# First feed-forward products over plain quarters, later conversions, and a gate product on VectorE

## The chip, the cores and the metric

The kernel runs on one core of one Trainium2 chip. The metric is the device time of one execution in microseconds. The figure for the kernel before is the median of three runs; the profile is of one more execution, with a time of its own.

## What is computed

The reference runs one inference step of a four-part decoder trunk on 1024 prompt rows and 64 sample rows (8 sequences of 8) of width 1024, in float32:

```python
for i in range(DEPTH):                       # DEPTH = 2
    mix = rglru_mixer(x, ...) if i % 2 == 0 else hgrn2_mixer(x, ...)
    x = layer_norm(ALPHA * x + mix, ln_g[i, 0], ln_b[i, 0])
    f = conv_ffn(x, ffn_conv[i], ffn_w_in[i], ffn_conv_w[i], ffn_conv_b[i], ffn_w_out[i])
    x = layer_norm(ALPHA * x + f, ln_g[i, 1], ln_b[i, 1])

def conv_ffn(x, buf, w_in, cw, cb, w_out):   # w_in is 1024 x 5632
    gate, up = jnp.split(x @ w_in, 2, axis=-1)
    gc, new_buf = causal_dwconv(gate, buf, cw, cb)
    return (jax.nn.gelu(gc) * up) @ w_out, new_buf

# in rglru_mixer, of 1024 channels in 8 heads of 128:
    r = jax.nn.sigmoid(gates[0]); ig = jax.nn.sigmoid(gates[1])
    log_a = RG_C * r * jax.nn.log_sigmoid(lam)
    a = jnp.exp(log_a)
    bvals = jnp.sqrt(jnp.maximum(-jnp.expm1(2.0 * log_a), 0.0)) * ig * xc
    _, h = lax.associative_scan(combine, (a, bvals), axis=1)
```

## The kernel before

**Numbers in two halves.** Every float32 operand of a product is kept as a high half (a cast by ScalarE, ACT in the profile) and a low half (the value minus the high half, a subtraction on GpSimd, POOL, or on VectorE, DVE). A product of two such operands is three products on TensorE (PE): high by high, high by low, low by high.

**Four phases.** Phase 0 is the RG-LRU mixer with its out-projection, phase 1 the first feed-forward layer, phase 2 the HGRN2 mixer, phase 3 the second feed-forward layer. `ffn` builds phases 1 and 3 with the same code. In the profile the start of phase 1 lies at about 348 us and that of phase 3 at about 1804 us, the same rows 1455.7 us later.

**The program is a list of steps** (`stepf`). Each step names weight blocks and a function. `blocks` holds all weight blocks in the order of use, and two things run ahead of the products along it. `issue_raw` starts loads of float32 weights into free raw buffers (raw0, raw1, in a feed-forward layer rawf0, rawf1 too), on SyncE's queue (SP); L140 is the load. `convert` turns what is loaded into high and low halves in a weight tile (wb0, wb1, wb2, wxf0, each of two halves). A raw buffer returns to `rawq` when the conversion of its whole block is written. `pump`, which `products` and `ln_pipeline` call, writes such conversions and pending work into the program; so the place of a conversion in each engine's queue is decided when the program is written, and every engine takes its queue in order.

**In-projection of a feed-forward layer.** Steps alternate: `gates` of a pair of 128-column blocks (f0, f1), then `ups` of the same pair. `products` multiplies a pair by a scheme of seven products over quarters: the rows of x are cut in two halves of 512, the inner dimension in two halves of 512, the pair in its two blocks. The seven left sides are sums and differences of quarters of x, xc[0] to xc[6], of which xc[0], [3], [4] and [6] are used by the change. The seven right sides are sums and differences of weight quarters, made by `convert_part`: four of the seven parts need one more subtraction or addition on POOL (L176, L178, L180, L182) before the cast (L185) and the low half (L186). Each product is 12 matmuls (4 inner tiles by 3), and is done for two chunks of rows, c = 0 with n = 288 (256 prompt rows and 32 sample rows) and c = 1 with n = 256. That is 2 x 7 x 12 = 168 matmuls for a pair. In a first pair, `order` in `products` takes all seven products of c = 0 ahead of those of c = 1; in later ones the two chunks alternate. Results go from PSUM to row-long slots by copies on ACT and additions on DVE in `evac` (L1103, L1110, L1118).

**How x comes to its quarters.** `ln_pipeline` runs over nine row tiles in the order 8, 0, 4, 1, 5, 2, 6, 3, 7 (8 holds the sample rows): the last out-projection products of the tile, then `pump()`, then in `nrm_a` the square of the centred rows on ACT (L455) with its sum, then on DVE the scale and shift. `to_sums(mp)` for mp = 0 to 3 transposes the tiles mp and mp + 4 on PE (L375) and makes xc of them: ACT writes the high halves (L402), POOL three of the low ones (L406), and in `late()` POOL subtracts (L427), ACT casts and POOL subtracts again for xc[5]. Chunk c = 0 needs mp 0 and 1, chunk c = 1 needs mp 2 and 3. The last one, `to_sums(3)`, is left pending, and `flush` writes it into the middle of the first pair's products.

**RG-LRU.** For each of eight heads `rg_a`, `rg_b`, `rg_c` follow one another in `pend`: on ACT exponential and tanh, on DVE L873, L875 and L876 over 128 x 1112 elements, on ACT the square root L882, on POOL the product of input gate and convolved row L883 (in `rg_b`), on DVE its product with the square root L893, then the scans L900 and L901.

**Last out-projection group of a feed-forward layer.** Four weight blocks of 256 rows x 512 columns: (f0, columns 0), (f0, columns 1), (f0+2, columns 0), (f0+2, columns 1). They are converted by `convert` with their low halves on the engine that `run["lo"]` names (POOL in these phases, L217).

## Time and profile before

| | |
|---|---|
| median of 3 runs | 2586.22 us (2585.59 to 2587.18) |
| profiled execution, its own time | 2582.2 us |
| span in the profile | 2580.4 us |
| PE busy in the span | 2492.6 us, 97% |
| DVE, ACT, POOL busy | 1551.0, 955.3, 1415.4 us |
| mean granted clock of TensorE | 0.989 of full speed |

The profiled execution is 4.0 us shorter than the median, and its span 1.8 us shorter than its time. PE is idle for 88 us of the span. In the chain that ended last, PE's products have the greatest shares, and DVE, POOL and ACT together 7%.

### The profile page before, as it was taken

Reading aid. Unit: us, or ns where it says so; the run is one execution under the profiler, and the core shown is the slowest. Engines: PE = TensorE matmul, PEld = TensorE weight load, DVE = VectorE, ACT = ScalarE, POOL = GpSimd, SP = SyncE. Lnnn points to the kernel's source line nnn. Section 1 sums busy time; section 2 is a strip of 40 time slices with the busy share of each in tenths; the row PEclk is TensorE's granted clock in tenths of the full one; section 3 lists DMA queues with packets and bytes.
Section 4 is the critical chain, followed back from the end, with each engine's and each line's share of the span. In section 5 each row is a group of like instructions: output and inputs, shape, how many; then the busy total and the mean of one; then the engine's idle time right before and its main releaser. Section 6 shows DMA issues by size and latency. Waiting matters only on the chain. (4 is left out here: it accounts for less than half of the span.)

```text
span 2580.4 us, 39885 instructions
## 1 busy us (share of the span) xinstructions
PE 2492.6 (97%) x16007; PEld 2306.8 (89%) x16007; DVE 1551.0 (60%) x2367; ACT 955.3 (37%) x1653; POOL 1415.4 (55%) x1179
## 2 busy tenths in 40 slices
PE   9999979999999999999999999999799999999997
PEld 9998869999999788799999999877799999988886
DVE  5998375665655422468858485977556565662327
ACT  4776243333333211244545353444333333340113
POOL 2664168888886532115544453614788888872321
PEclk9999989999999999999999999999999999999999
DMA  4114121222224422121211111122222222264112
GB/s 133 41 46 149 50 82 59 80 80 85 67 85 146 177 101 84 48 83 42 60 34 50 51 43 51 43 93 97 74 85 67 85 67 89 71 243 142 61 38 73
DMA packets 205839, 209.79 MB, mean 81 GB/s; under 512 B 13201, under 2 KB 167953, under 8 KB 205614
## 3 DMA queue, kind: packets, MB, share of 16 engines
q1 hardware_dynamic: 205654, 207.25, 25.0%
q8 instruction: 126, 2.06, 0.3%
q14 instruction: 59, 0.48, 0.1%
HBM read 159.61 MB, written 47.61 MB: 80 GB/s over the span
## 5 line engine op out<-in xcount | busy, mean ns | idle before, releaser
L217 POOL TENSOR_TENSOR wb<-raw,wb 128x1024 fp32r<-128x1024 f32 (+1 forms) x76 | 202.4, 2666 | 493.3 <-ACT wb L216 273.2
L1103 DVE TENSOR_TENSOR z<-z,ps_f 128x256 f32<-128x256 f32 (+2 forms) x550 | 195.9, 378 | 363.6 <-PE ps_f L1098 295.0
L1098 PE MATMUL ps_f<-xa,wb 128*128 128x288 f32 (+1 forms) x3072 | 397.5, 289 | 11.6 <-POOL wb L186 4.7
L1098 PEld LDWEIGHTS ps_f<-xa,wb 128*128 128x128 f32 x3072 | 390.1, 188 | 14.2 <-POOL wb L186 5.6
L1098 PE MATMUL ps_f<-x,wb 128*128 128x288 f32 (+1 forms) x2496 | 325.6, 291 | 0.3 <-ACT z L1110 0.3
L1098 PEld LDWEIGHTS ps_f<-x,wb 128*128 128x128 f32 x2496 | 321.2, 190 | 1.1 <-ACT z L1110 1.1
L300 PE MATMUL ps_in<-xa,wb 128*128 128x384 f32 (+3 forms) x912 | 307.4, 337 | 13.2 <-ACT y8h L1391 5.9
L301 PE MATMUL ps_in<-xa,wb 128*128 128x384 f32 (+3 forms) x912 | 300.5, 330 | 0.3 <-DVE xa L358 0.3
L302 PE MATMUL ps_in<-xa,wb 128*128 128x384 f32 (+3 forms) x912 | 300.5, 329 | 0.1
L444 DVE SCALAR_TENSOR_TENSOR z<-z,ps_fo 128x512 f32<-128x512 f32 x128 | 87.4, 685 | 290.3 <-PE ps_fo L1203 281.7
L186 POOL TENSOR_TENSOR wb<-rawf,wb 128x512 fp32r<-128x512 f32 x116 | 165.6, 1436 | 57.0 <-ACT wb L185 55.5
L186 POOL TENSOR_TENSOR wb<-raw,wb 128x512 fp32r<-128x512 f32 x116 | 162.9, 1410 | 60.6 <-ACT wb L185 50.4
L300 PEld LDWEIGHTS ps_in<-xa,wb 128*128 128x128 f32 x912 | 173.6, 190 | 17.9 <-ACT y8h L1391 7.3
L1151 DVE SCALAR_TENSOR_TENSOR z<-z,ptf 128x1104 f32<-128x1104 f32 x88 | 182.3, 2071 | 1.6
L301 PEld LDWEIGHTS ps_in<-xa,wb 128*128 128x128 f32 x912 | 173.6, 190 | 1.3 <-DVE xa L358 0.7
L302 PEld LDWEIGHTS ps_in<-xa,wb 128*128 128x128 f32 x912 | 173.2, 190 | 1.1 <-DVE wb L217 0.5
L216 ACT CAST wb<-raw 128x1024 fp32r<-128x1024 f32 (+1 forms) x81 | 79.7, 986 | 233.7 <-issue 117.5
L1098 PE MATMUL ps_f<-xa,wxf 128*128 128x256 f32 (+1 forms) x1152 | 149.8, 288 | 2.4 <-ACT z L1118 2.4
L1098 PEld LDWEIGHTS ps_f<-xa,wxf 128*128 128x128 f32 x1152 | 146.6, 188 | 2.8 <-ACT z L1118 2.8
L185 ACT CAST wb<-rawf 128x512 fp32r<-128x512 f32 x116 | 71.0, 623 | 208.2 <-POOL rawf L182 76.0
L185 ACT CAST wb<-raw 128x512 fp32r<-128x512 f32 x116 | 70.4, 624 | 187.2 <-POOL raw L182 63.7
L1201 PE MATMUL ps_fo<-wb,xa 128*128 128x512 f32 x320 | 126.4, 395 | 2.4 <-DVE z L444 2.4
(510 smaller groups left out, 5710.9 us busy)
## 6 DMA issues: line engine op xcount, KB each, us to landing
raw<-in_ffn_w_in_dram SPq DMA_DIRECT2D x44, 512.0 KB
rawf<-in_ffn_w_in_dram SPq DMA_DIRECT2D x44, 512.0 KB
ysave<-z SPq DMA_DIRECT2D x44, 512.0 KB
raw<-in_hg_w_in_dram SPq DMA_DIRECT2D x32, 512.0 KB
xa<-ysave SPq DMA_DIRECT2D x28, 544.0 KB
zsave<-z SPq DMA_DIRECT2D x24, 512.0 KB
raw<-in_ffn_w_out_dram SPq DMA_DIRECT2D x24, 512.0 KB
z<-zsave SPq DMA_DIRECT2D x24, 512.0 KB
```

The lines of the kernel that those rows point to most:

```text
L185: act.copy(w[:, 0], src)
L186: run["lo"].tensor_tensor(w[:, 1], src, w[:, 0], ALU.subtract)
L216: act.copy(w[:, 0, :n], raw[:, :n])
L217: run["lo"].tensor_tensor(w[:, 1, :n], raw[:, :n], w[:, 0, :n], ALU.subtract)
L300: pe.matmul(ps[:, :n], lhsT=wh, rhs=xh, start=(k == 0), stop=False)
L301: pe.matmul(ps[:, :n], lhsT=wh, rhs=xl, start=False, stop=False)
L302: pe.matmul(ps[:, :n], lhsT=wl, rhs=xh, start=False, stop=(k == KT - 1))
L444: dve.scalar_tensor_tensor(zz, zz, a, ps, ALU.mult, ALU.add, accum_out=stat[:, m, n:n + 1] if acc else None)
L1098: pe.matmul(ps[:, :n], lhsT=l, rhs=r, start=(kk == 0 and i < 4 and l is wh and r is xh), stop=(kk == 3 and l is wl), skip_group_check=(i > ...
L1103: dve.tensor_tensor(d, s, pv(ps), ALU.add)
L1151: dve.scalar_tensor_tensor(c[:, :L], gs[:, i:i + L], w[:, i:i + 1], c[:, :L], ALU.mult, ALU.add)
L1201: pe.matmul(ps, lhsT=yh, rhs=wh, start=a, stop=False)
```

## The change

1. **First gates block of each feed-forward layer.** It has the kind "q": four parts, which are its four quarters as they are. `products_first` multiplies them by xc[0], xc[3], xc[4], xc[6] in eight products for each chunk, 192 matmuls for the pair in place of 168. Within a chunk it does f0 whole and then f1. For each of both, xc[0] and xc[3] meet the first quarter in two PSUM banks, then xc[4] and xc[6] meet the second quarter in the same two banks. The first bank is copied to its place after the first product and again after the third, and the second bank is added after the fourth. `flush` comes after f0 of chunk 0.
2. **Place of conversions.** In the last tile of `ln_pipeline` `pump()` stands behind `nrm_a` and `late()`. In the second pass of the mixer's out-projection a call of `convert()` is taken out.
3. **`rg_b`.** The product of input gate and convolved row is on DVE.
4. **Last out-projection group.** The blocks stand in the order (f0, columns 0), (f0+2, columns 0), (f0, columns 1), (f0+2, columns 1), and the low halves that are made at the end of the group before are on DVE.
5. `products` loses its argument `first`.

```diff
@@ class Block @@
+            self.parts = 1 if len(loads) == 1 else 4 if kind == "q" else 7
@@ convert_part @@
-        if i == 1:
+        if b.parts == 4:
+            src = (a11, a12, a21, a22)[i]
+        elif i == 1:
             pool.tensor_tensor(a21, a11, a21, ALU.subtract)
...
@@ ln_pipeline @@
         for i, m in enumerate(order):
             step_m(m)
-            pump()
+            if i < NT - 1:
+                pump()
             nrm_a(m, junk())
             late()
+            if i == NT - 1:
+                pump()
@@ mix_out, second pass @@
-                        if n == 1:
-                            convert()
@@ rg_b @@
-        pool.tensor_tensor(ig[:, :W], ig[:, :W], st["xc"][:, :W], ALU.mult)
+        dve.tensor_tensor(ig[:, :W], ig[:, :W], st["xc"][:, :W], ALU.mult)
@@ ffn @@
+        def products_first(b, places):
+            for f, (get, pieces) in enumerate(places):
+                get()
+            for c in range(2):
+                c0, n = HCH[c]
+                for f, (get, pieces) in enumerate(places):
+                    q1, q2 = pieces(0, c), pieces(1, c)
+                    banks = [psi.tile([P, 512], F32, name="ps_f", tag="in") for _ in range(2)]
+                    for h, xs in enumerate(((0, 3), (4, 6))):
+                        while len(b.w) <= 2 * f + h:
+                            assert convert(), "no place for weights"
+                        w = b.w[2 * f + h][0]
+                        for ps, i in zip(banks, xs):
+                            for kk in range(4):
...
+                                    pe.matmul(ps[:, :n], lhsT=l, rhs=r, start=(h == 0 and kk == 0 and l is wh and r is xh),
+                                              stop=(kk == 3 and l is wl), skip_group_check=(h == 1))
+                            if i == 0:
+                                for d, pv in q2:
+                                    act.copy(d, pv(ps))
+                            elif i == 4:
+                                for d, pv in q1:
+                                    act.copy(d, pv(ps))
+                            elif i == 6:
+                                for d, pv in q2:
+                                    dve.tensor_tensor(d, d, pv(ps), ALU.add)
+                        pump()
+                    if c == 1:
+                        put_half(b.w[2 * f][1])
+                        put_half(b.w[2 * f + 1][1])
+                        pump()
+                    if c == 0 and f == 0:
+                        flush()
...
-            order = [(i, c) for c in range(2) for i in range(7)] if first else [(i, c) for i in range(7) for c in range(2)]
-            for i, c in order:
+            for i, c in [(i, c) for i in range(7) for c in range(2)]:
...
+                            if gi + 2 == len(GROUPS):
+                                run["lo"] = dve
...
                     flush()
+                    run["lo"] = pool
...
-                        prod(m, 0, grp, [ws[0], ws[2]], False, True)
+                        prod(m, 0, grp, ws[:2], False, True)
...
-                stepf(phase, [out_blk(WO, f0, 0), out_blk(WO, f0, 1), out_blk(WO, f0 + 2, 0), out_blk(WO, f0 + 2, 1)], fn, "cccc")
+                stepf(phase, [out_blk(WO, f0 + 2 * i, n) for n in range(2) for i in range(2)], fn, "cccc")
```

Three queues show where instructions stand around the first gates block. In all of them xa_68, x45 and x6 are parts of xc, z_69 the rows and slots, ps_t transposed rows, ps_f results of products.

This is ACT's queue before, from the last casts of `to_sums(2)` to the first conversions of the block after:

```order
L402 CAST xa_68<-z_69 128x4x128 x3
L185 CAST wb0_84<-raw0_82 128x512
L185 CAST wb0_84<-raw1_83 128x512
L402 CAST x45_0_2500<-z_69 128x4x128
L1110 COPY z_69<-ps_f_2982 128x256
L1110 COPY z_69<-ps_f_2982 128x4x8
L185 CAST wxf0_2975<-raw0_82 128x512
L185 CAST wxf0_2975<-rawf00_2973 128x512
```

And this is the same stretch after, where L406, L189, L1103 and L1106 are the cast of xc, the cast of weights and the two copies out of the first bank:

```order
L406 CAST xa_68<-z_69 128x4x128 x3
L189 CAST wb2_86<-raw1_83 128x512
L189 CAST wb0_84<-raw0_82 128x512
L406 CAST x45_0_2500<-z_69 128x4x128
L189 CAST wb0_84<-raw1_83 128x512
L1103 COPY z_69<-ps_f_2982 128x256
L1103 COPY z_69<-ps_f_2982 128x4x8
L189 CAST wxf0_2975<-raw1_83 128x512
L1106 COPY z_69<-ps_f_2982 128x256
L1106 COPY z_69<-ps_f_2982 128x4x8
L189 CAST wxf0_2975<-raw0_82 128x512
```

After the change the cast out of raw1 in the second row is the fourth and last part of the gates block. The two casts into wb0_84 belong to the ups block, whose loads come after that part, and both stand ahead of the first copy out of ps_f_2982.

SP's queue before has the two loads of the ups block into rawf0 and rawf1, behind the last of nine stores of the rows (L488):

```order
L140 DMA raw0_82<-in_ffn_w_in_dram 128x8x128
L140 DMA raw1_83<-in_ffn_w_in_dram 128x8x128
L488 DMA zsave_80<-z_69 64x1024
L488 DMA zsave_80<-z_69 128x1024 x8
L140 DMA rawf00_2973<-in_ffn_w_in_dram 128x8x128
L140 DMA rawf01_2974<-in_ffn_w_in_dram 128x8x128
```

SP's queue after has them in raw0 and raw1, ahead of the last store (L492):

```order
L141 DMA raw0_82<-in_ffn_w_in_dram 128x8x128
L141 DMA raw1_83<-in_ffn_w_in_dram 128x8x128
L492 DMA zsave_80<-z_69 64x1024
L492 DMA zsave_80<-z_69 128x1024 x7
L141 DMA raw0_82<-in_ffn_w_in_dram 128x8x128
L141 DMA raw1_83<-in_ffn_w_in_dram 128x8x128
L492 DMA zsave_80<-z_69 128x1024
```

The ups block is loaded into the buffers that the gates block has just left, one store earlier in the queue.

POOL's queue before, in the same stretch:

```order
L178 TENSOR_TENSOR raw1_83<-raw1_83 128x512
L186 TENSOR_TENSOR wb2_86<-raw1_83,wb2_86 128x512
L180 TENSOR_TENSOR raw0_82<-raw1_83,raw0_82 128x512
L186 TENSOR_TENSOR wb2_86<-raw0_82,wb2_86 128x512
L406 TENSOR_TENSOR xa_68<-z_69,xa_68 128x4x128 x3
L186 TENSOR_TENSOR wb0_84<-raw0_82,wb0_84 128x512
L186 TENSOR_TENSOR wb0_84<-raw1_83,wb0_84 128x512
L427 TENSOR_TENSOR z_69<-z_69 128x512
L406 TENSOR_TENSOR x45_0_2500<-z_69,x45_0_2500 128x4x128
```

POOL's queue after (L190 is the low half of a weight part, L410 that of a part of xc, L179 a combination of weight quarters):

```order
L190 TENSOR_TENSOR wb2_86<-raw1_83,wb2_86 128x512
L410 TENSOR_TENSOR xa_68<-z_69,xa_68 128x4x128 x3
L190 TENSOR_TENSOR wb2_86<-raw1_83,wb2_86 128x512
L190 TENSOR_TENSOR wb0_84<-raw0_82,wb0_84 128x512
L431 TENSOR_TENSOR z_69<-z_69 128x512
L410 TENSOR_TENSOR x45_0_2500<-z_69,x45_0_2500 128x4x128
L179 TENSOR_TENSOR raw1_83<-raw0_82,raw1_83 128x512
L190 TENSOR_TENSOR wb0_84<-raw1_83,wb0_84 128x512
```

The two combinations of the gates block are gone. The fourth part's low half, the second L190 row, stands behind three low halves of `to_sums(2)`, and the first combination of the ups block (L179) is in the stretch.

## Rows read from the trace of the kernel before

**Rows 1.** The page, busy time, share of the span and instructions by engine.

```profile
PE 2492.6 (97%) x16007; PEld 2306.8 (89%) x16007; DVE 1551.0 (60%) x2367; ACT 955.3 (37%) x1653; POOL 1415.4 (55%) x1179
```

**Rows 2.** Windows: busy us of each engine, then granted clock, DMA share, GB/s.

```profile
100.00:200.00 100.00, 92.40 (x545) 91.06 (x543) 97.31 (x76) 70.84 (x96) 63.41 (x38) 0.97 0.17 48
300.00:400.00 100.00, 82.75 (x469) 71.24 (x468) 69.12 (x129) 44.59 (x99) 59.93 (x47) 0.93 0.20 67
```

**Rows 3.** Single lines: duration ns (min/median/max), first and last start, forms.

```profile
L883 POOL TENSOR_TENSOR z<-z x8: 2600/3739/4579, 66.3 to 205.8; 128x1112 f32<-128x1112 f32 x8
L875 DVE SCALAR_TENSOR_TENSOR z<-z x8: 1316/3498/3519, 70.2 to 209.7; 128x1112 f32<-128x1112 f32 x8
L873 DVE TENSOR_TENSOR z<-z x8: 1300/1304/3775, 66.3 to 206.1; 128x1112 f32<-128x1112 f32 x8
```

**Rows 4.** Timeline of POOL and DVE in one head: start, duration, instruction.

```profile
86.54 3.74 POOL L883 TENSOR_TENSOR z<-z 128x1112 f32<-128x1112 f32 x1
...
87.94 3.51 DVE L875 SCALAR_TENSOR_TENSOR z<-z 128x1112 f32<-128x1112 f32 x1
```

**Rows 5.** PE's waits in 160 to 215, a clock window, an ACT row there.

```profile
PE ps_in L300 <- ACT z L856: 5.0, 2, 4.8
PE ps_ri L854 <- POOL xcs L842: 2.6, 2, 2.4
...
200.00:202.00 2.00, 2.00 (x6) 2.00 (x7) 2.00 (x2) 2.00 (x5) 2.00 (x1) 0.50 0.00 0
...
195.98 1.13 ACT L882 ACTIVATE z<-z 128x1112 f32<-128x1112 f32 x1 [6.10 <-DVE z L876]
```

**Rows 6.** Timeline of ACT, and one DVE row, in the first gates block of phase 1.

```profile
351.08 0.21 DVE L454 TENSOR_SCALAR stat<-stat 128x1 f32<-128x1 f32 x1
...
357.94 0.62 ACT L185 CAST wb<-raw 128x512 fp32r<-128x512 f32 x1 [3.46 <-POOL raw L180]
358.47 1.14 ACT L455 ACTIVATE junk<-z,stat 128x1024 f32<-128x1024 f32 x1
...
360.17 0.57 ACT L402 CAST xa<-ps_t 128x512 fp32r<-128x512 f32 x1
...
364.47 1.14 ACT L402 CAST xa<-z 128x512 fp32r<-128x512 f32 x2 [0.83 <-DVE z L418]
...
377.97 0.58 ACT L402 CAST xa<-ps_t 128x512 fp32r<-128x512 f32 x1
...
386.71 0.62 ACT L402 CAST x<-z 128x512 fp32r<-128x512 f32 x1 [3.36 <-POOL z L427]
```

**Rows 7.** Timeline of PE in the same stretch, and its wait at the ups.

```profile
351.51 3.71 PE L1098 MATMUL ps_f<-xa,wb 128*128 128x288 f32 x26
...
372.22 1.97 PE L375 MATMUL ps_t<-ident,z 128*128 128x128 f32 x8 [7.80 <-DVE z L483]
374.36 5.39 PE L1098 MATMUL ps_f<-x,wb 128*128 128x288 f32 x24 [0.17 <-ACT z L1110]
...
392.10 1.56 PE L1098 MATMUL ps_f<-x,wxf 128*128 128x256 f32 x12
393.50 3.16 PE L1098 MATMUL ps_f<-xa,wxf 128*128 128x288 f32 x24
...
PE ps_f L1098 <- ACT z L1118: 2.1, 2, 1.2
```

**Rows 8.** SP's load of a raw buffer, and POOL's first use of it.

```profile
297.19 0.37 SPq L140 DMA_DIRECT2D raw<-in_ffn_w_in_dram  x1
...
301.12 1.29 POOL L176 TENSOR_TENSOR raw<-raw,raw 128x512 f32<-128x512 f32 x1 [2.70 <-DMA raw<-in_ffn_w_in_dram]
```

**Rows 9.** Last out-projection group of phase 3: PE, POOL, and a conversion on DVE elsewhere.

```profile
2518.24 0.50 PE L1207 MATMUL ps_fo<-wxb,x 128*128 128x512 f32 x1 [1.29 <-POOL wxb L217]
...
2515.82 2.37 POOL L217 TENSOR_TENSOR wxb<-raw,wxb 128x1024 fp32r<-128x1024 f32 x1 [23.97 <-ACT wxb L216]
1684.78 1.21 DVE L217 TENSOR_TENSOR wb<-raw,wb 128x1024 fp32r<-128x1024 f32 x1
```

## What I expect of the change

> **What bounds the kernel now.** I read the page's first table first: PE is busy 97% of the span [rows 1]. So the kernel is bound by PE nearly everywhere, and what a change is worth is decided in the few stretches where PE idles or runs at half its clock. The view by windows then names the stretches that this change touches [rows 2]. In 100 to 200 us, in the RG-LRU, PE is busy 92.40 of 100 us while DVE is busy 97.31: there DVE sets the pace. In 300 to 400, which holds the first gates block of phase 1, PE is busy 82.75 at a granted clock of 0.93, and no other engine passes 70: there PE waits for a chain across engines. Phase 3 repeats that block, so a price there counts twice. Last I read the waits and the timelines of both places and of the last out-projection group.
>
> About 0.2% (5.2 us) is what a measurement of this kernel can tell from no change.
>
> **The gate product on DVE.** L883 on POOL takes 3739 ns in the median, and L875 on DVE takes 3498 in the median but 1316 at its shortest, for the same elements [rows 3]. The timeline shows why: L883 starts at 86.54 and L875, inside that time, at 87.94, and both end about together [rows 4]. So L883 costs DVE about 3.50 - 1.32 = 2.18 us in each of eight heads, sometimes taken from L873 (longest 3775) instead, 17.4 us in all. The product on DVE costs what L873, also a product of two such tiles, costs undisturbed: 1.30 each [rows 3], 10.4 in all. DVE gets 7.0 back. Is that PE's time? In 160 to 215 PE waits 5.0 and 2.6 us, and the longer comes from ACT, which had itself waited 6.10 for DVE's L876; after it the clock is at its lower level, 0.50 in 200 to 202 [rows 5]. The mean clock of 0.97 over 100 us [rows 2] makes some 3 us more. PE can thus win at most 5.0 + 2.6 + 3 = 10.6. DVE's 7.0 fits under it, and I take **-7.0**, between -3 (the two short waits by POOL stay, and part of the saving falls where DVE does not lead) and -10.6.
>
> The Trainium skill, "SBUF — State Buffer", section "Who interferes with whom", says that VectorE and GpSimd share a pair of ports, that a VectorE instruction with two inputs in SBUF contends with a GpSimd instruction that reads SBUF, and that the loser blocks for the whole instruction; the pair of rows at 86.54 and 87.94 looks like that. "Perfetto Trace Analysis", section "Optimizing Scalar/DVE Operations", speaks against the move: as both share a read port, moving operations between these two might not help. By that rule this term would be 0 and not -7.0; the case stands among the rivals.
>
> **The first gates block.** The changed block makes eight products for each chunk instead of seven: 24 matmuls more, 12 of n = 288 (26 of them take 3.71 us, 0.143 each) and 12 of n = 256 (1.40 from the start at 392.10 to that at 393.50) [rows 7], together 1.7 + 1.4 = 3.1 us. Two combinations on POOL go, and the square of the last rows comes first. Before, its statistic was ready at 351.3, but the square stood behind two casts that waited for POOL's combinations (the second until 357.94) and began at 358.47 [rows 6], 7.1 us late. That is the gain meant to pay for the 3.1.
>
> I replayed the block by the queues, in the time base of before. PE begins at 351.5 as now, with 24 matmuls, f0's xc[0] and xc[3] on the first quarter: done at 351.5 + 24 x 0.143 = 354.9. The next product, xc[4], goes into the bank that holds the first result, so it needs the copy of that bank by ACT. In ACT's queue this copy stands behind the last casts of `to_sums(2)`, behind xc[5]'s cast, and behind two casts of the *ups* block. The second of those needs raw1 loaded anew and a combination on POOL (L179). When is that?
> - Square at 351.3; from its start to the first cast of `to_sums` 360.17 - 358.47 = 1.7 [rows 6]; a weight cast of 0.6 between: first cast at 353.6.
> - Of `to_sums(3)`, where nothing else stands in the queues, the first cast is at 377.97 and xc[5]'s at 386.71 after a wait for POOL's L427 [rows 6]: 8.7. L427 itself takes about 1.3, by the 1.29 of a POOL operation of this size [rows 8]. So the three low halves of `to_sums(2)` end 7.4 after the first cast, at 361.0.
> - Then POOL has the fourth part's low half (362.3), the ups block's first low half (363.6), xc[5]'s subtraction (364.9), ACT's cast of 0.6, xc[5]'s low half (366.8), and only then L179.
> - Raw1's load waits for the fourth part's low half, 362.3. Between the issue of such a load at 297.19 and POOL's first use of it at 301.12 lie 3.9 us [rows 8]: 366.2.
>
> So L179 starts at about 367.0 (366 to 369.5: the low halves could stretch, as DVE works on the last rows at that time). Then 1.3 for L179, 0.6 for the cast, 0.5 for the copy: PE goes on at 369.4, after **14.5 us** of idling. The casts of `to_sums(2)` take 364.47 + 1.14 - 360.17 = 5.4 us [rows 6], so without the ups casts the copy would have come at about 360.
>
> Next, 24 matmuls after such a wait take 5.39, as now at 374.36 behind a wait of 7.80, and the transposes of `to_sums(3)` 1.97 [rows 7]: 376.8. Its first cast comes at 375.9, xc[5]'s cast 8.7 later at 384.6. Behind that stands the copy of f1's first bank: 384.6 + 0.6 + 0.5 = 385.7, whereas PE has done f1's first 24 by 380.2. It idles **5.5 us** again, then 24 at 5.39 (391.1) and eight products of n = 256 at 1.40 (11.2): the ups start at 402.3. Now they start at 393.50 [rows 7]: +8.8. The two waits of the ups for ACT, 2.1 now [rows 7], may go or stay, since their conversions come earlier; I take 0.8 off. **+8.0 for each layer, +16 for both**, with bounds of +4 (L179 a microsecond sooner, the second wait without a slower clock, both waits of the ups gone) and +11.5 (L179 at 369.5, nothing off).
>
> The call of `convert()` that is removed, and `pump()` behind the square, lie in this replay already. SP's queue now holds the ups loads ahead of the last store of rows, which delays only that store; nothing reads those rows before the out-projection. I cost this at nothing.
>
> **The last out-projection group.** PE waits 1.29 us there for the low half of a weight block, which POOL makes in 2.37 [rows 9]. The same conversion on DVE took 1.21, and the blocks now come in the order of use. I take the wait as gone in both layers: **-2.6** (0 if DVE, which adds the residuals there, comes to it late; -3.2 with the odd tenths behind it).
>
> **Sum.** -7.0 + 16.0 - 2.6 = +6.4 us. On the profiled execution's own time of 2582.2 that is 2588.6. The median of the runs is 4.0 above that execution, so the forecast is 2586.2 + 6.4 = **2592.6 us**. Its own range, from the bounds that can meet, is 2586 to 2602.
>
> **Rivals.**
> - *POOL comes to L179 much sooner* (the other side). The added wait hangs on one chain on POOL and one load. With the casts of `to_sums(2)` alone ahead of it, the copy would come at about 360, and each microsecond that L179 is earlier is one less for each layer. The change is faster by over 5.2 us if L179 starts before about 361. With a start at 358 the layer gives -1.0 instead of +8.0 and the sum is -7.0 - 2.0 - 2.6 = -11.6, **2574.6 us**. For it: that square's 7.1 us. Against it: four POOL operations that the queue puts ahead, and a load that cannot start before the low half of the fourth part.
> - *The wait is there, but short*: +3.0 a layer, about the price of the added matmuls, if raw1 and POOL arrive some 5 us sooner, or the second wait does not occur since `to_sums(3)` starts early. -7.0 + 6.0 - 2.6 = -3.6, **2582.6 us**, no change that can be told. For it: before, the block idles already, 7.80 in one place [rows 7], so that some of the new waiting replaces old.
> - *The move to DVE brings nothing*: the RG-LRU's pace stays, because DVE's gained time is filled or PE's waits come from POOL's and ACT's part of the chain. 0 + 16.0 - 2.6 = +13.4, **2599.6 us**. For it: DVE gets 1.30 more to do in each head, in the engine that is busy 97.31 of 100. Against it: the 2.18 that it loses now.
>
> **How the numbers follow.** The forecast 0.50, POOL sooner 0.12, short wait 0.25, nothing from the move 0.13. Faster by over 0.2% (under 2581.0) are the first rival and a quarter of the second: 0.18. Slower by over 0.2% (over 2591.4) are the third and three quarters of the forecast's own: 0.51. The rest, 0.31, is no change. The range of 2578 to 2603 leaves out most of the first rival and the upper end of the third.
>
> **What would show it.** In the profile after: DVE's L875 at 1.3 in all heads, a product of 1.3 of its own, and shorter waits of L300 and L854 in 160 to 215. In the gates block the square directly behind its statistic; on PE a wait of 12 to 17 us for ACT's copy after the first 24 matmuls, ended by a cast that waited for POOL's combination of the ups block; a second one of about 5 after `to_sums(3)`; the ups 51 us after the block's first product, where 42.0 lie between them now [rows 7]. No wait for a low half in the last out-projection group. The forecast is wrong if PE's first wait is under 8 us, or if L875 stays at 3.5, or if the blocks after, whose conversions are now earlier or later, start to wait where they do not now.

## The result and the profile after

The changed kernel takes 2604.45 us in the median of four runs (2599.52 to 2606.37), the kernel before 2585.9 beside it: a ratio of 1.0068, with a 95% interval of 1.005 to 1.0085. That is 18.6 us slower. The forecast was 6.4 slower and its range ended 1.5 us short of the result. The profiled execution took 2603.26, 21.1 more than that of before, and the numbers below are read from it. The profile overstates the loss by 2.5 us, since the execution of before that was profiled lies 3.7 below the median of its kernel and that of the changed kernel 1.2. One run of a kernel below, that with an even count of halves, took 6305.07 us, in a state apart from all others, and its median leaves it out.

The page of the changed kernel, as [rows 1]:

```profile
PE 2502.3 (96%) x16055; PEld 2318.3 (89%) x16055; DVE 1522.3 (59%) x2359; ACT 964.8 (37%) x1659; POOL 1363.4 (52%) x1155
```

PE has 48 matmuls more, 9.7 us more of busy time and a longer span; POOL lost 52 us of work. PE's idle time grew from 88 to 99 us, so half of the added time is work or a slower clock and half is waiting.

**RG-LRU.** Single lines of the changed kernel, duration in ns (least, median, most), as [rows 3]; L880 was L875, L878 was L873, and L888 is the product that moved. Then its window as [rows 2], and PE's waits in 160 to 215 as [rows 5]:

```profile
L880 DVE SCALAR_TENSOR_TENSOR z<-z x8: 1316/1318/1318, 68.7 to 203.3; 128x1112 f32<-128x1112 f32 x8
L888 DVE TENSOR_TENSOR z<-z x8: 1307/1308/1310, 70.7 to 205.3; 128x1112 f32<-128x1112 f32 x8
L878 DVE TENSOR_TENSOR z<-z x8: 1303/1310/1331, 67.3 to 201.9; 128x1112 f32<-128x1112 f32 x8
...
100.00:200.00 100.00, 95.90 (x575) 95.01 (x574) 89.88 (x81) 75.52 (x103) 51.24 (x33) 1.00 0.15 43
...
PE ps_in L304 <- ACT z L861: 2.8, 1, 2.8
PE ps_ri L859 <- POOL xcs L847: 0.9, 1, 0.9
```

None of the three lines is stretched any more, DVE is busy 89.88 where it was 97.31, PE's two long waits have shrunk, and in this execution the clock stays at its higher level. (In the run with the gate product alone, below, the same window has 0.98.)

**First gates block of phase 1.** The timeline of PE, then of ACT and POOL, as [rows 6, 7]:

```profile
344.69 3.45 PE L1099 MATMUL ps_f<-xa,wb 128*128 128x288 f32 x24
364.11 5.29 PE L1099 MATMUL ps_f<-x,wb 128*128 128x288 f32 x24 [15.97 <-ACT z L1103]
369.24 1.91 PE L379 MATMUL ps_t<-ident,z 128*128 128x128 f32 x16
370.90 3.43 PE L1099 MATMUL ps_f<-xa,wb 128*128 128x288 f32 x24
380.13 5.77 PE L1099 MATMUL ps_f<-x,wb 128*128 128x288 f32 x24 [5.79 <-ACT z L1103]
...
397.10 6.20 PE L1140 MATMUL ps_f<-xa,wb 128*128 128x288 f32 x48
...
344.51 1.15 ACT L459 ACTIVATE junk<-z,stat 128x1024 f32<-128x1024 f32 x1 [1.96 <-DVE stat L458]
...
359.87 0.62 ACT L406 CAST x<-z 128x512 fp32r<-128x512 f32 x1 [6.46 <-POOL z L431]
363.08 0.62 ACT L189 CAST wb<-raw 128x512 fp32r<-128x512 f32 x1 [2.59 <-POOL raw L179]
363.61 0.45 ACT L1103 COPY z<-ps_f 128x256 f32<-128x256 f32 x2
...
351.73 3.47 POOL L410 TENSOR_TENSOR xa<-z,xa 128x512 fp32r<-128x512 f32 x2 [0.18 <-ACT xa L406]
...
357.60 2.24 POOL L431 TENSOR_TENSOR z<-z 128x512 f32<-128x512 f32 x1
360.57 1.26 POOL L410 TENSOR_TENSOR x<-z,x 128x512 fp32r<-128x512 f32 x1 [0.73 <-ACT x L406]
361.79 1.26 POOL L179 TENSOR_TENSOR raw<-raw,raw 128x512 f32<-128x512 f32 x1
```

The block begins 6.8 us earlier than before (344.69 against 351.51): that is the RG-LRU's gain in this execution. The square starts as its statistic is ready. Then PE stops for 15.97 us in front of f0's third product, and for 5.79 in front of f1's. What ends the first wait is the copy L1103, and the rows of ACT show what stands ahead of it: xc[5]'s cast, which waited 6.46 for POOL, and a cast of the ups block, which waited 2.59 for POOL's combination L179. From the first gates product to the ups it now takes 52.4 us, 42.0 before.

**First out-projection group of phase 1.** Here y, the result of the layer's inner part, meets the weights of the out-projection (the out blocks). PE's waits there, then POOL's conversions of out blocks (L221) between the low halves of y (L1224), then a window:

```profile
843.00 0.50 PE L1242 MATMUL ps_fo<-wb,xa 128*128 128x512 f32 x1 [0.50 <-POOL wb L221]
845.33 0.50 PE L1243 MATMUL ps_fo<-wb,xa 128*128 128x512 f32 x1 [1.13 <-POOL xa L1224]
852.58 0.50 PE L1242 MATMUL ps_fo<-wb,xa 128*128 128x512 f32 x1 [0.92 <-POOL wb L221]
863.97 0.80 PE L1241 MATMUL ps_fo<-wb,xa 128*128 128x512 f32 x1 [2.96 <-DVE z L448]
...
836.83 2.77 POOL L1224 TENSOR_TENSOR xa<-xa 128x1024 fp32r<-128x1024 f32 x2 [6.80 <-ACT xa L1223]
839.57 3.38 POOL L221 TENSOR_TENSOR wb<-rawf,wb 128x1024 fp32r<-128x1024 f32 x1
842.90 7.28 POOL L1224 TENSOR_TENSOR xa<-xa 128x1024 fp32r<-128x1024 f32 x4
850.14 2.38 POOL L221 TENSOR_TENSOR wb<-raw,wb 128x1024 fp32r<-128x1024 f32 x1
...
860.00:870.00 10.00, 7.04 (x19) 5.26 (x18) 6.77 (x8) 0.00 (x0) 6.99 (x6) 0.66 1.00 380
```

And the same place in the kernel before, which the prediction had not looked at (L217 is the conversion, L1184 the low halves of y):

```profile
843.59 0.50 PE L1203 MATMUL ps_fo<-wb,xa 128*128 128x512 f32 x1 [1.08 <-POOL xa L1184]
859.43 0.50 PE L1201 MATMUL ps_fo<-wb,xa 128*128 128x512 f32 x1 [1.33 <-DVE z L444]
...
828.96 2.39 POOL L217 TENSOR_TENSOR wb<-raw,wb 128x1024 fp32r<-128x1024 f32 x1 [3.06 <-ACT wb L216]
837.44 7.37 POOL L1184 TENSOR_TENSOR xa<-xa 128x1024 fp32r<-128x1024 f32 x4 [4.75 <-ACT xa L1183]
...
860.00:870.00 10.00, 10.00 (x44) 8.08 (x43) 9.51 (x11) 0.00 (x0) 6.37 (x4) 1.00 1.03 372
```

Before, the second out block was converted at 828.96, ahead of all low halves of y; now its conversion stands at 839.57, behind two of them. Two waits for low halves of out weights are new (0.50 and 0.92), the one for the residual is 1.6 us longer, and behind it the granted clock is down to 0.66 over ten microseconds (0.51, the lower level, from 863 to 870). In phase 3 the waits come again (0.49, 0.93 and 1.89), but not the fall of the clock. In the later groups of each layer two more waits for low halves of out weights, of some 0.4 us each, are new; the even count of halves, below, leaves these in place.

The starts of the same PE instructions in the two profiles show where the 21 us are. The "second set" is the first matmul of the out-projection's fourth row tile (859.43 and 863.97 above, 2314.86 and 2335.27 in phase 3). The first out-projection product starts at 839.79 and 840.72, in phase 3 at 2295.46 and 2313.07.

| from | to | before, us | after, us | difference |
|---|---|---|---|---|
| start | first gates product, phase 1 | 351.5 | 344.7 | -6.8 |
| first gates product | ups, phase 1 | 42.0 | 52.4 | +10.4 |
| ups | first out-projection product, phase 1 | 446.3 | 443.6 | -2.7 |
| first out-projection product | second set, phase 1 | 19.6 | 23.3 | +3.6 |
| second set | first gates product, phase 3 | 947.8 | 953.4 | +5.6 |
| first gates product | ups, phase 3 | 42.0 | 52.1 | +10.1 |
| ups | first out-projection product, phase 3 | 446.3 | 443.6 | -2.7 |
| first out-projection product | second set, phase 3 | 19.4 | 22.2 | +2.8 |
| second set | end of span | 265.5 | 266.1 | +0.6 |

Below, the *long stretch* is the time from the second set of phase 1 to the last transposes ahead of phase 3's gates block: 946.7 us before, 952.4 after.

### The profile page after: what moved, and what is told of

Same layout as the page of the kernel before. It is cut to its first block, busy times and chain, and to the rows that moved or that the text cites. A ratio compares the mean times of both kernels' runs of the same rounds, so it can differ in the third digit from the quotient of the medians.

```text
span 2601.4 us, 39929 instructions
## 1 busy us (share of the span) xinstructions
PE 2502.3 (96%) x16055; PEld 2318.3 (89%) x16055; DVE 1522.3 (59%) x2359; ACT 964.8 (37%) x1659; POOL 1363.4 (52%) x1155
## 5 line engine op out<-in xcount | busy, mean ns | idle before, releaser
L221 POOL TENSOR_TENSOR wb<-raw,wb 128x1024 fp32r<-128x1024 f32 (+1 forms) x76 | 204.4, 2691 | 522.3 <-ACT wb L220 390.5
L1145 DVE TENSOR_TENSOR z<-z,ps_f 128x256 f32<-128x256 f32 (+2 forms) x520 | 187.8, 380 | 367.6 <-PE ps_f L1140 312.9
L1140 PEld LDWEIGHTS ps_f<-xa,wb 128*128 128x128 f32 x3120 | 395.5, 188 | 0.0
L1140 PE MATMUL ps_f<-x,wb 128*128 128x288 f32 (+1 forms) x2160 | 279.3, 289 | 0.0
L1140 PEld LDWEIGHTS ps_f<-x,wb 128*128 128x128 f32 x2160 | 275.5, 189 | 0.0
L190 POOL TENSOR_TENSOR wb<-raw,wb 128x512 fp32r<-128x512 f32 x124 | 177.4, 1437 | 101.7 <-ACT wb L189 100.2
L190 POOL TENSOR_TENSOR wb<-rawf,wb 128x512 fp32r<-128x512 f32 x104 | 144.6, 1393 | 56.6 <-ACT wb L189 42.0
L189 ACT CAST wb<-raw 128x512 fp32r<-128x512 f32 x124 | 75.4, 620 | 185.2 <-POOL raw L185 48.0
L1503 POOL TENSOR_TENSOR z<-z 128x256 f32<-128x256 f32 x144 | 96.9, 705 | 51.5 <-DVE z L1476 30.6
L1241 PE MATMUL ps_fo<-wb,xa 128*128 128x512 f32 x288 | 115.2, 400 | 4.9 <-DVE z L448 4.9
L1242 PE MATMUL ps_fo<-wb,xa 128*128 128x512 f32 x288 | 115.5, 401 | 3.6 <-POOL wb L221 3.6
L1140 PE MATMUL ps_f<-xa,wxf 128*128 128x256 f32 (+1 forms) x912 | 118.2, 288 | 0.0
```

The lines of the kernel that those rows point to most:

```text
L190: run["lo"].tensor_tensor(w[:, 1], src, w[:, 0], ALU.subtract)
L221: run["lo"].tensor_tensor(w[:, 1, :n], raw[:, :n], w[:, 0, :n], ALU.subtract)
L1140: pe.matmul(ps[:, :n], lhsT=l, rhs=r, start=(kk == 0 and i < 4 and l is wh and r is xh), stop=(kk == 3 and l is wl), skip_group_check=(i > ...
L1145: dve.tensor_tensor(d, s, pv(ps), ALU.add)
L1241: pe.matmul(ps, lhsT=yh, rhs=wh, start=a, stop=False)
L1242: pe.matmul(ps, lhsT=yh, rhs=wl, start=False, stop=False)
```

## The experiments

Each was timed beside the kernel before on its chip, in five rounds.

**The gate product alone.**

```diff
-        pool.tensor_tensor(ig[:, :W], ig[:, :W], st["xc"][:, :W], ALU.mult)
+        dve.tensor_tensor(ig[:, :W], ig[:, :W], st["xc"][:, :W], ALU.mult)
```

> The kernel before with one line of the change, the gate product of rg_b on VectorE. The prediction's theory, VectorE gets back 2.18 us a head and pays 1.30: about 7 us faster, 2579 against 2586, and the first gates block begins some 6.8 us earlier with its inner times unchanged. Rival, the two engines only exchange work: no difference, 2584 to 2588.

2580.88 against 2585.3, ratio 0.998 (0.9971 to 0.999): 4.4 us faster, between 2.6 and 7.5. In its profile the gates begin at 344.99 and the block takes 42.0 as before. The two engines do not only exchange work.

**All but the quarters.** The changed kernel with `products` and seven combined parts for the first gates block, so with parts 2, 3 and 4 of the change.

```diff
-            pump()
+            if i < NT - 1:
+                pump()
             nrm_a(m, junk())
             late()
+            if i == NT - 1:
+                pump()
...
-                        if n == 1:
-                            convert()
```

> All of the change but its first part: the first gates block keeps its seven combined products. If the added time is the quarters' (the copy of the first bank behind conversions of the ups block, and an odd count of weight halves that makes the first out-projection group wait), then 2571 to 2578: -6.8 from the RG-LRU, -2.0 from the last out-projection group, 0 to -4 a layer from the earlier square, and no wait for a weight's low half at the first out-projection group. Rival, the later conversions (part 2) or the order of the last group cost the time: 2590 to 2600, with PE waiting longer for low halves in the gates block or with the waits of the first out-projection group still there.

2573.89 against 2585.3, ratio 0.9957 (0.9944 to 0.997): 11.4 us faster. The gates blocks take 39.5 and 39.0, and the first out-projection group has no new wait. So the loss lies in the first part of the change, and the others together gain. PE's rows in the gates block show why the squares gain only 2.5 here:

```profile
351.52 1.58 PE L1099 MATMUL ps_f<-xa,wb 128*128 128x288 f32 x10 [1.51 <-POOL wb L186]
359.58 0.85 PE L1099 MATMUL ps_f<-xa,wb 128*128 128x288 f32 x2 [6.48 <-ACT wb L185]
```

A weight cast that stood ahead of the square now stands behind `to_sums(2)`'s casts, and PE waits 6.48 for it in place of the 7.80 for the rows.

**Conversions of the ups block held.** The changed kernel; `convert` leaves the first ups block alone until f0's second copy is in ACT's queue.

```diff
         b = blocks[run["cvt"]]
+        if b.held:
+            return False
...
                             elif i == 4:
                                 for d, pv in q1:
                                     act.copy(d, pv(ps))
+                                fs_["held"].held = False
...
```

> The changed kernel, but no part of the ups block is converted before f0's second copy is written into ScalarE's queue. Queue theory: the copy loses the two casts ahead of it and stands behind the cast of xc[5] alone, so PE's first wait falls from 16.0 to about 11.5 and the ups start some 4 to 6 us earlier in each layer: 2593 to 2597 against 2604. Rival, the wait is set by the chain that makes xc[5] or by the load alone: 16 us as before, 2604.

2596.46 against 2585.3, ratio 1.0044 (1.003 to 1.0058). PE's rows in the block:

```profile
344.67 3.45 PE L1102 MATMUL ps_f<-xa,wb 128*128 128x288 f32 x24
358.70 6.13 PE L1102 MATMUL ps_f<-x,wb 128*128 128x288 f32 x24 [10.58 <-ACT z L1106]
...
391.54 6.20 PE L1144 MATMUL ps_f<-xa,wb 128*128 128x288 f32 x48
```

The first wait falls from 15.97 to 10.58 and the block to 46.9. The casts of the ups block made 5.4 us of the wait; ahead of the copy now stands xc[5]'s cast, which the run with the copies first moves too.

**An even count of halves.** The changed kernel, and the third pair's ups block takes one half of a weight tile that stays empty, so that later blocks meet other tiles.

```diff
         b.w.append((w, item))
+        if b.ready and b.pads:
+            b.pad = get_half(b.phase == run["phase"])
...
+            blocks[-1].pads = p == 2
```

> The changed kernel, and one later ups block (the third pair's) holds one empty weight half beside its seven, so that the number of halves used up to the out-projection is even again (152 instead of 151; 154 before the change). Odd-half theory: the waits of the first out-projection group for low halves (0.5, 0.9 us and 3.0 or 1.9 us for the residual behind them, with a clock that falls in one layer) go, and two out blocks are converted ahead of the casts of y: 5 to 9 us faster than the changed kernel, 2595 to 2599; gates block unchanged. Rival, those waits come from VectorE's conversions, the last group's order or the loads: the same waits, 2604.

2597.2 against 2585.3, ratio 1.0049 (1.0036 to 1.0062). That is under the changed kernel by 7 us in the medians and by 5 in the ratios, whose intervals overlap; it is the rows that show the effect. Its rows at the first out-projection group:

```profile
848.56 0.50 PE L1249 MATMUL ps_fo<-wb,xa 128*128 128x512 f32 x1 [1.13 <-POOL xa L1230]
864.15 0.50 PE L1247 MATMUL ps_fo<-wb,xa 128*128 128x512 f32 x1 [1.07 <-DVE z L452]
```

The two waits for low halves are gone, the residual's is 1.07, and the clock does not fall there. From the ups to the second set it takes 463.0 and 463.3, 3.8 and 2.5 less than the changed kernel. The gates block is as slow as it was.

**An odd count in the kernel before.** The same edit on the kernel before, and nothing else.

> The kernel before, with one empty weight half held beside the seven of the third pair's ups block, so that the count of halves up to the out-projection is odd (155 instead of 154). Nothing else of the change is in it. Odd-half theory: one out block fewer is converted before the casts of y, and PE waits for low halves in the first out-projection group and longer for the residual behind it, 2 to 4 us in each layer, with more where the clock falls: 2590 to 2596 against 2586. Rival, the waits of the changed kernel need the other parts of the change: no such wait, 2586.

2585.94 against 2584.62, ratio 1.0004 (0.9995 to 1.0013): no difference. PE has one wait of 0.53 for a low half and a shorter one (0.69) for the residual. Oddness alone is not the cause; the expectation was wrong. The next run moves the out blocks further.

**Places of the out blocks close to the changed kernel's, in the kernel before.** The same edit, with one empty half in each of six ups blocks.

```diff
...
+            blocks[-1].pads = 2 <= p <= 7
```

> The kernel before, with one empty weight half held in each of six ups blocks (pairs three to eight), so that the out blocks meet the tiles in the changed kernel's places: one out block is converted ahead of the casts of y instead of two, the second, third and fourth come 10, 15 and 16 rows behind the first of these casts (6, 15 and 16 in the changed kernel; 2 rows ahead, 10 and 15 behind in the kernel before). The run with an odd count alone had one wait of 0.5 us there. Rotation theory: the waits of the changed kernel's first out-projection group come back without anything else of the change, 0.5 and 0.9 us for low halves and 1.5 to 3 us for the residual, so that this group begins its second bank set 2 to 4 us later than in the kernel before, counted from the first gates product (507.9 us there): 510 to 512, and 2587 to 2592 in all. Rival, they need the changed kernel's other parts: 508 and 2585.

2594.09 against 2585.23, ratio 1.0038 (1.0024 to 1.0052). PE waits for the low half of the second out block, once in each layer:

```profile
846.10 0.79 PE L1208 MATMUL ps_fo<-wb,xa 128*128 128x512 f32 x1 [4.07 <-POOL wb L221]
...
2308.26 0.79 PE L1208 MATMUL ps_fo<-wb,xa 128*128 128x512 f32 x1 [4.07 <-POOL wb L221]
```

From the first gates product to the second set it takes 510.9 (862.86 - 351.92; before 507.9). Without any other part of the change, the order in which tiles come free decides how many out blocks are converted ahead of the casts of y, and those converted behind them stop PE. The wait is 4.07 in one place and not 0.50 and 0.92 in two, since the second block comes ten rows behind the first cast of y and not six; behind it the granted clock is 0.72 over six microseconds, in phase 3 0.52. The total is 2 us over the expected, which had not counted the long stretch: it is 3.5 longer (950.2).

**The last out-projection group alone.** Part 4 of the change on the kernel before.

> The kernel before with the fourth part of the change alone (order of the last out-projection group, its low halves on VectorE). By the prediction's term the two waits of 1.29 and 0.25 us go in each layer: about 2.6 faster, 2583 against 2586; the changed kernel's trace has one wait of 0.55 left, so 2 at least. Rival, opened by the runs so far: the stretch from the first out-projection group of phase 1 to the first gates block of phase 3 is 3 to 6 us longer in all kernels with this part (949.9 to 952.4 against 946.8 and 947.2 without it), so this part costs phase 2 as much as it gains: no change or 1 to 3 us slower, and that stretch at 950 or more.

2582.99 against 2584.62, ratio 0.9992 (0.9983 to 1.0). One wait of 0.55 is left in each layer where 1.29 and 0.25 stood, so 1.0 a layer in the profile; the timed 1.6 us are not clear of no change. The long stretch is 947.3, so the rival falls.

**The squares alone.** Part 2 on the kernel before.

> The kernel before with the second part of the change alone (conversions behind the last square, none in the middle of the second pass). The run without the quarters took 39.5 and 39.0 us from the first gates product to the ups (42.0 before): so 2.5 to 3 us gained in each layer's block. In phase 2's stretch either 947 as before, then 2579 to 2581 in all, or 949.7 to 951, then this part gives back there 3 to 4 of what it gains: 2582 to 2584.

2576.83 against 2585.23, ratio 0.9965 (0.9953 to 0.9978): 8.4 faster, more than expected; the blocks take 39.5 and 39.0, 5.5 less than before, and the long stretch 947.2. Where the rest comes from is not shown: its profiled execution is only 4.7 faster than that of before.

**The copies first.** The changed kernel with an even count of halves, the ups block held until f1's second copy, and xc[5] of both last row pairs made behind the copies.

```diff
                             elif i == 4:
                                 for d, pv in q1:
                                     act.copy(d, pv(ps))
+                                if c == 0:
+                                    late()
+                                    if f == 1:
+                                        fs_["held"].held = False
...
                 to_sums(m - 4)
-                if m == order[-1]:
-                    late()
...
         nrm_c(order[-1], final)
-        late()
...
```

> The changed kernel with an even count of halves, ups conversions held until f1's second copy, and xc[5] of both last row pairs made behind the second copy of f0 and of f1, so that the copies of the first bank stand behind nothing but casts that PE needs as well. Queue theory: f0's copy comes right after the fourth part's cast, PE's first wait falls from 16.0 to 5 or 6 us, the second from 5.7 to 2 or 3, the ups start some 14 to 17 us earlier than in the changed kernel (36 to 39 us after the block's first product, where the kernel before takes 42.0): 2565 to 2572, under both kernels. Rival, the eight products cannot win since the ups' conversions come too late then, or the first chunk's chain is as long without the queue: PE waits for weights at the ups instead, 2580 or more.

2572.72 against 2584.62, ratio 0.9948 (0.9935 to 0.996): faster than both kernels, by 12 and by some 32 us. PE's rows:

```profile
348.18 3.44 PE L1103 MATMUL ps_f<-xa,wb 128*128 128x288 f32 x24
356.60 5.95 PE L1103 MATMUL ps_f<-x,wb 128*128 128x288 f32 x24 [4.99 <-ACT z L1107]
...
369.22 3.47 PE L1103 MATMUL ps_f<-x,wb 128*128 128x288 f32 x24 [1.72 <-ACT z L1107]
...
384.25 3.12 PE L1103 MATMUL ps_f<-x,wb 128*128 128x256 f32 x24 [3.08 <-ACT z L1107]
387.20 6.18 PE L1148 MATMUL ps_f<-xa,wb 128*128 128x288 f32 x48
```

The same eight products take 39.0 us with the copies in front. The waits fall as expected and a little further, to 4.99 and 1.72. A new one of 3.08 in the second chunk, for a copy behind casts of the ups block, keeps the blocks at 39.0 and 40.3, at or just over the end of what was expected.

**The same, with the squares first only in the mixers.** At a feed-forward layer's end `pump()` stands ahead of the last square again.

> The run with the copies first, and conversions stand behind the last square only in the mixers' pipelines; at the end of a feed-forward layer they are ahead of it, as in the kernel before. All kernels with conversions behind the last square took 949.7 to 952.9 us from the second bank set of phase 1's out-projection to the first gates block of phase 3, those without it 946.7 to 947.3. If the feed-forward's end is the cause: 947, and 2.5 us faster than the run with the copies first (2570 against 2572.7). If not: 949.5 to 950.5 again and no difference.

2570.87 against 2585.23, ratio 0.9944 (0.9931 to 0.9956), which is the run above within the intervals. The long stretch is 951.3: the feed-forward's end is not what lengthens it.

## Why the prediction was wrong

*RG-LRU, -7.0.* Right in its mechanism. DVE's lines are at 1.3, and in the profile the gates begin 6.8 earlier; the timed runs of that line alone give -4.4 (-2.6 to -7.5). It is partly luck that 6.8 is so close to 7.0: in the profiles of the other kernels with this line the block begins at 344.67 to 348.18, 3.3 to 6.8 earlier than before, and the later it begins the more the lower clock has taken ahead of it (1.7 us at 344.67, 5.1 at 348.18). One reading was loose: the pair of rows at 86.54 and 87.94 does not end together, DVE's ends 1.17 later (91.45 against 90.28), which is nearly the 1.32 that it takes undisturbed. The Trainium skill's "Perfetto Trace Analysis", section "Optimizing Scalar/DVE Operations", says that moving operations between these two engines might not help. Here it did, by the 4.4 us of the run with that line alone. The rival that the move brings nothing falls.

*First gates block, +8.0 a layer.* Right in mechanism, and in size by two misses that cancel. Forecast were waits of 14.5 and 5.5, measured 15.97 and 5.79; the block is 10.4 and 10.1 longer, not 8.8, because POOL's L431 took 2.24, not 1.3, and two low halves ahead of it 3.47, where `to_sums(3)` takes some 2.5. In the trace of before the same operation, L427 there, is as slow in `to_sums(2)`, at 371.05, and fast in `to_sums(3)`, whose rows the replay took:

```profile
371.05 2.25 POOL L427 TENSOR_TENSOR z<-z 128x512 f32<-128x512 f32 x1
...
385.38 1.29 POOL L427 TENSOR_TENSOR z<-z 128x512 f32<-128x512 f32 x1
```

The waits of the ups for ACT (2.1 us), of which the sum took 0.8 off, went away whole, and the time from the ups to the out-projection fell by 2.7. Together this is some 7.7 and 7.5 a layer, against 8.0. What the copy waited for was the chain on POOL that the replay named, xc[5] and L179; holding the ups casts takes off 5.4 of the 16, and putting xc[5] behind as well another 5.6. So the copy "at about 360" without the ups casts left out xc[5]'s cast, which the same paragraph has in the queue: PE goes on 14.0 us after the block's start when the ups casts are held (365.5 in the prediction's time), and 8.4 after it (359.9) only when xc[5] is behind too. Neither POOL sooner nor a short wait occurred.

*Last out-projection group, -2.6.* Right in sign, -2.0 in the profile: one wait of 0.55 stays in each layer. In the timed runs of that part alone it is -1.6 and not clear of nothing.

*The sum.* This step failed. It added what happens up to the ups and in the last out-projection group, and took everything between as unchanged; the one sentence on blocks "whose conversions are now earlier or later" stood as a warning without a price. By the terms as measured in the profile the change would cost -6.8 + 15.2 - 2.0 = +6.4, as forecast. The profile shows 21.0 more in the span, so 14.6 lie elsewhere:

- 6.4 in the first out-projection group, 3.6 in phase 1 and 2.8 in phase 3, by the waits for low halves and the residual. Four weight halves instead of seven shift the tiles that all later blocks meet. The even count of halves takes the waits for low halves away and brings the residual's back to 1.07 and 1.34, and the kernel before loses 8.9 us when its out blocks alone are moved to similar places. In the timed medians the even count takes some 7 us off (2604.45 against 2597.2).
- 3.0 by the lower clock right behind the residual's wait in phase 1, at the start of the long stretch; the run with an even count, where that wait is 1.07, did not have it.
- 3.6 in the rest of the long stretch (its 5.6, and the 1.0 that the last group gains in it, less these 3.0). PE's idle time in the stretch is the same (22.4 us in both), and the lower clock takes 3.4 us more there (last section); why is open.
- 1.6 behind the second set of phase 3 (its 0.6, and the 1.0 gained by the last group), where two of the new waits of 0.4 lie.

*The count of matmuls* was costed right and is small: 24 more made 3.1 us of the block's 10. With the copies first, the block with eight products is as short as the one with seven and the squares first (39.0 and 40.3, against 39.5 and 39.0), so on these two kernels the quarters neither gain nor lose.

## What to carry to other kernels

A conversion that a planner writes early takes a place in an engine's queue, and whatever stands behind it waits for its loads and its helpers; look for the instruction that frees a PSUM bank and keep it ahead of work that nobody needs yet. A change in how many buffers one block takes moves every later block to other buffers: replay the next place where whole buffers are needed, here 450 us later. Here the replay gave its stage to within a microsecond, in part since two misses cancelled, and the error lay in the stages that were left out.

## What was not expected of the hardware

The long stretch came out short in some profiles and long in others. In the kernel before, and with one part of the change alone (the gate product, the last group, the squares), and with an odd count, it took 946.7 to 947.3 us; in the kernels with several parts 949.7 to 952.9, and 950.2 in the kernel before with the changed places. PE's idle time in it is 21.1 to 22.5 us in all of them. What differs is the granted clock. Summed over the stretch, the time that the lower level (0.50 in the trace) takes away, half of the time spent at it, is 6.8 us in each of the five short ones and 10.2 to 13.7 in the seven long ones. The windows 1240 to 1700 of the run with the gate product alone, of the run without the quarters, of the run with the squares alone, of the kernel before and of the changed kernel:

```profile
1240.00:1700.00 460.00, 442.09 (x2958) 415.05 (x2956) 335.29 (x569) 213.65 (x329) 213.82 (x218) 0.99 0.15 44
1240.00:1700.00 460.00, 442.43 (x2942) 416.52 (x2941) 330.14 (x558) 212.20 (x327) 202.95 (x215) 0.97 0.15 44
1240.00:1700.00 460.00, 442.14 (x2962) 416.75 (x2962) 336.78 (x569) 212.40 (x329) 214.96 (x219) 0.99 0.15 44
1240.00:1700.00 460.00, 442.22 (x2963) 416.88 (x2963) 336.35 (x568) 211.88 (x329) 214.55 (x219) 0.99 0.15 44
1240.00:1700.00 460.00, 442.70 (x2961) 419.10 (x2959) 335.70 (x567) 212.34 (x332) 217.52 (x228) 0.98 0.15 44
```

PE's busy time is the same to 0.6 us, and the clock is 0.99 in the short ones and 0.97 and 0.98 in the long ones; a hundredth of 460 us is 4.6. What brings the clock down there is not shown: of its six falls in the changed kernel between 1240 and 1700, three have no wait of PE of half a microsecond in the 20 us ahead of them. No single part of the change that was run alone gives the long side, but each length is that of one execution. The mean granted clock of a kernel also varies between executions (0.985 to 0.991 in the timed runs of the kernel before, which took 2580.87 to 2590.81 us). Whether the kernel or the execution decides, and why the combined kernels are on the long side, stays open.
